# Token statistics of a conv and recurrence layer: squares summed over every eighth token, 1/rms stored without a turn by TensorE

## Chip, core and metric

The kernel runs on one core of one Trainium2 chip. The metric is device time in microseconds (us) of one execution. Before the change the median of 3 runs is 727.97 us (727.86 to 728.05). Engines are named as in the profile: PE is TensorE's matmul, PEld its weight load, DVE VectorE, ACT ScalarE, POOL GpSimd, SP SyncE, which issues most DMAs.

## What is computed

One layer over 1024 tokens of 1024 channels, batch 1. A token's 1/rms scales all channels of that token; the change lies in how this one number per token is made and spread.

```python
h = rmsnorm(x, norm_g) * (1.0 + scale) + shift      # scale, shift, gate from silu(c) @ mod_w + mod_b
u = h @ w_in                                        # five groups of 1024 columns
cv, cg, cs, lx, ls = jnp.split(u, ...)
...                                                 # gated causal conv (31 taps), layernorm, projection
...                                                 # causal conv (4 taps), gates, linear recurrence
y = jnp.concatenate([y_conv, y_lru], axis=-1) @ w_out
x = x + (1.0 + gate) * y
return rmsnorm(x, final_g)
```

with `rmsnorm(x, g) = x * rsqrt(mean(x * x, axis=-1) + EPS) * g`.

## The kernel before

Channels stand on the 128 partitions and tokens along the free dimension. x arrives as eight tiles of 128 channels x 1024 tokens (`xt[k]`). Each f32 product is made of three matmuls: both operands are split into a high part (`whi`, `uh`) and a rest (`wlo`, `ul`), and hi x hi, hi x rest and rest x hi are summed in one PSUM bank of 512 columns. Weights come by DMA (`raw`), ScalarE casts the high part (`whi`), VectorE or GpSimd subtracts for the rest (`wlo`).

The first column tiles of u don't wait for the norm. `uh`, `ul` (line 875) are x times the channel's gain alone, and the products of `first` (line 790, seven banks over four column tiles, and `late` for the eighth) and of the three tiles in `NEXT` (line 505, `ps`) are multiplied by 1/rms of the token afterwards, on VectorE, by the row `rbc` that holds the 1024 values on every partition. Those results are `first_u` (lines 1310 and 1318) and `next` (line 1359). Then VectorE scales x itself by `gs` and `rbc` (line 997), ScalarE and VectorE make the full h from it in two parts (again `uh`, `ul`, lines 1006 and 1008), and all later tiles of u read these. `fsum` (line 970) and `psbias` (line 985) make the part of u that comes from shift.

The statistics (lines 918 to 951): ScalarE squares the eight tiles of x, VectorE adds them into one tile `sq` of 128 partitions x 1024 tokens. `stats` (line 932) then sums over partitions: eight f32 matmuls, in each of which 128 token columns of `sq` are the stationary operand and a column of ones moves, so that the sums of block b stand in column b of `psb` (named token_stats), token p of the block on partition p. ScalarE takes the root (line 940, `st`, 128x8), VectorE the reciprocal (line 942). `turn` (line 944) is a matmul with `st` as stationary operand against the identity matrix: it puts block b on partition b, 8x128, in the same bank. ScalarE copies this to SBUF (line 948) and issues the DMA that stores it in DRAM as a row of 1024 in token order (line 949); SyncE issues the DMA that reads that row onto all 128 partitions, `rbc` (line 950).

The order of work isn't the program's order. `S.op` collects operations with their engine, a cost, a priority, and what they read and write; `Plan.order` (line 174) plays a list schedule over all of them with those costs and sets the order of the whole program on each engine. An operation that goes, or gets another cost or predecessor, therefore can move others anywhere behind it. On the chip only semaphores for real dependences hold; `after=` and priorities act on the order alone.

Of the kernel before, what the change touches and what calls it, by code (L numbers as in the profile page):

```python
# [9 lines left out]
F32 = mybir.dt.float32  # L10
# [4 lines left out]
P = 128  # L15
D = 1024
T = 1024
KT = D // P
# [72 lines left out]
SQP, RSP, BIP, HHP, HCH, EVP = -84, -110, -50, -56, 0.1, -80  # L91
# [25 lines left out]
class Plan:  # L117
# [14 lines left out]
    @staticmethod  # L132
    def keys(items):
        for it in items:
            if isinstance(it, tuple):
                yield it
            else:
                for i in range(it.parts):
                    yield (it, i)
# [162 lines left out]
def hymba_layer(ctx: ExitStack, tc: tile.TileContext, xT, xa, vecs, mod_w, w_first, w_pairs, w_in,  # L302
# [3 lines left out]
    act, dve, pool, pe, sp = nc.scalar, nc.vector, nc.gpsimd, nc.tensor, nc.sync  # L306
# [7 lines left out]
    dram = ctx.enter_context(tc.tile_pool(name="dram", bufs=1, space=bass.MemoryType.DRAM))  # L314
# [11 lines left out]
    S = Plan(pools)  # L326


    def a_cost(n, ptr=0):
        return 0.1 + 0.00083 * n + 0.09 * ptr  # L330
# [7 lines left out]
    def ACT(prio, out, in_, func, n=T, bias=None, scale=None, accum=None, r=(), w=(),  # L338
            reserve=0, after=()):
        kw = {}  # L340

        def emit():
            if func == "copy":
                act.copy(out(), in_())  # L344
                return
            if bias is not None:
                kw["bias"] = bias
            if scale is not None:
                kw["scale"] = scale
            if accum is not None:  # L350
                kw["accum_out"] = accum
            act.activation(out=out(), in_=in_(), func=func, **kw)  # L352
        ptr = sum(x is not None and not isinstance(x, float) for x in (bias, scale))
        return S.op("ACT", a_cost(n, ptr) + (0.1 if accum is not None else 0), emit, prio, r, w,
                    table=SETS.get(func), reserve=reserve, after=after)
# [33 lines left out]
    def DMA(prio, out, in_, nbytes, r=(), w=(), after=(), reserve=0):  # L389
        cost = max(0.1, nbytes / (EARLYRATE if prio < -94.5 + KT * 3.3 else 360e3))  # L390
        cost = FIRSTCOST.get(round(prio), cost) if prio < -96 else cost
        return S.op("SP", cost, lambda: sp.dma_start(out(), in_()), prio, r, w, after=after,
                    reserve=reserve)
# [7 lines left out]
    def big_buf(name, dt=F32, parts=1):  # L401
        return S.buf("big", name, dt, parts)

    def bank(name):
        return S.buf("bank", name)
# [5 lines left out]
    def part(b, a, e):  # L411
        if isinstance(b, Two):
            z = a // H
            return part(b.b[z], a - z * H, e - z * H)
        return lambda: b()[:, a:e]

    def halves(b, a, e):
        if isinstance(b, Two):
            return [(b.b[z], 0) for z in (0, 1) if z * H < e and a < z * H + H]
        return [(b, i) for i in range(b.parts) if i * (T // b.parts) < e  # L420
                and a < (i + 1) * (T // b.parts)]

    FULL_BYTES = P * T * 4
# [9 lines left out]
    ident = const.tile([P, P], F32, tag="ident", name="ident")  # L433
    make_identity(nc, ident)
    ones = const.tile([P, P], F32, tag="ones", name="ones")
# [6 lines left out]
    def ctile(name, n):  # L442
        return const.tile([P, n], F32, tag=name, name=name)
# [296 lines left out]
    psb = bank("token_stats")  # L740
# [16 lines left out]
    for i in range(IDLE):  # L757
        if i == IDLE0:
            for z, (a, e) in enumerate(CPARTS):
# [3 lines left out]
             after=[spread_op] if i >= IDLE0 else [])  # L763
# [9 lines left out]
    def fw_keys(b, k, a=0, e=FW):  # L773
        o, n = (k % 2) * FW, T // b.parts
        return [(b, j) for j in range((o + a) // n, (o + e - 1) // n + 1)]
# [27 lines left out]
    for i, ld in enumerate(LOADS):  # L803
        p = due[ld] = i - 100.0
# [5 lines left out]
        elif ld[0] in "wW":  # L810
# [6 lines left out]
                w=keys(rw))  # L817
            for j in range(k, k + nk):
# [3 lines left out]
                for a, e in ((0, FW // 2), (FW // 2, FW)) if j == 0 else ((0, FW),):  # L822
                    ACT(p, fw_part(hi, j, a, e), fw_part(rw, j, a, e), "copy", e - a, r=[(rw, jj)],
                        w=fw_keys(hi, j, a, e))
                if j:
                    SUB(p, "DVE", fw_part(lo, j), fw_part(rw, j), fw_part(hi, j), FW,
                        r=[(rw, jj), *fw_keys(hi, j)], w=fw_keys(lo, j))
# [31 lines left out]
    for k in range(KT):  # L859
        p = due[f"s{k}"]  # L860
# [13 lines left out]
        p = max(p, due[f"x{k}"] if k else p, due[f"w{k}"])  # L874
# [4 lines left out]
        for a, e in START if k < UK else ((0, T),):  # L879
            n = e - a  # L880
            hk = halves(x_, a, e)
            if k == 0 == a:
                o = TS(p, part(uh, a, e), part(x_, a, e), g, None, ALU.mult, n=n,
                       r=hk + [("gs", k)], w=halves(uh, a, e))
            else:
                o = ACT(p, part(uh, a, e), part(x_, a, e), AF.Copy, n, scale=g,
                        r=hk + [("gs", k)], w=halves(uh, a, e))
            if k == 0 == a:
                rw, hi, lo = fw[0]
                for b in (0, FW // 2):  # L890
                    z = b + FW // 2
                    SUB(p, "DVE", fw_part(lo, 0, b, z), fw_part(rw, 0, b, z), fw_part(hi, 0, b, z), z - b,
                        r=[(rw, 0), *fw_keys(hi, 0, b, z), *halves(uh, a, e)], w=fw_keys(lo, 0, b, z))
# [3 lines left out]
                r=hk + halves(uh, a, e) + [("gs", k)], w=halves(ul, a, e)))  # L897
# [10 lines left out]
        for ch, (a, e) in enumerate(START):  # L908
            for i, ps in enumerate(psf):
                if (a, e) not in cuts[i] or k == 0 == a:  # L910
                    continue
                q = p + 0.1 * ch if k < LASTK else due[f"w{KT - 1}"] + 0.01 * ((i + 1) % 4) + 0.001 * ch
                for z in range(3) if k < ZK else (None,):
                    o = fw_mm(q + 0.003 * (z or 0), ps, i, uh, ul, k, ((a, e),),
                              after=[begun[i, a // H]] if k == 0 and a % H else [], z=z)
# [3 lines left out]
    for k in range(KT):  # L919
        p = SQP + k  # L920
        sq = big_buf(f"sq{k}")
        ACT(p, sq, xt[k], AF.Square, r=[xt[k]], w=[sq], after=[scaled[k]])
        if k:
            to = sqs[0]
            TT(p, SUM[k], to, to, sq, ALU.add, r=[to, sq], w=[to],
               after=[last_split[k + SQD]] if k <= SQK else [])
        else:
            sqs.append(sq)
    rbc = big_buf("rbc", parts=4)
    st, wk = ctile("st", KT), [psb]  # L930

    def stats(sq, k):
        for b in range(KT):
            pe.matmul(psb()[:, b:b + 1], sq()[:, b * P:b * P + P], ones[:, 0:1],
                      start=k == 0 and b == 0, stop=k == len(sqs) - 1, skip_group_check=True)

    for k, sq in enumerate(sqs):
        S.op("PE", 0.23 * KT, lambda sq=sq, k=k: stats(sq, k), RSP, [sq], wk, columns=4 * P * KT,
             after=[last_u[LASTK - 1, 3, 0]] if k else [])
# [1 line left out]
               scale=1.0 / D, r=wk, w=[("st", 0)])  # L941
    S.op("DVE", 0.2, lambda: dve.reciprocal(st, st), RSP, [("st", 0)], [("st", 0)])

    def turn():
        pe.matmul(psb()[:KT, P:2 * P], st, ident, start=True, stop=True)
    spread = S.op("PE", 0.2, turn, RSP, [("st", 0)], wk, columns=4 * P)
    row, flat = lambda: rbc()[:KT, :P], dram.tile([KT, P], F32, tag="rrow", name="rrowd")
    spread_out = ACT(RSP, row, lambda: psb()[:KT, P:2 * P], "copy", P, r=wk, w=[(rbc, 0)])
    S.op("ACT", 0.3, lambda: act.dma_start(flat, row()), RSP, [(rbc, 0)], [("rrowd", 0)], lag=0.1)
    DMA(RSP, rbc, lambda: flat.rearrange("b p -> (b p)").partition_broadcast(P), FULL_BYTES,  # L950
        r=[("rrowd", 0)], w=[rbc])


# [4 lines left out]
    for k in range(KT):  # L958
        p = due[f"h{k}"]
# [6 lines left out]
        if k == 0:  # L966
            ACT(p, facc, fw_part(rw, k), AF.Copy, FW, scale=shift[:, k:k + 1],
                r=[(rw, 0), ("shift", k)], w=[(fsum, 0)])
# [3 lines left out]
        for i, s in enumerate(NEXT):  # L972
            to, rw = part(fsum, FW + i * P, FW + i * P + P), raw[s]
            src = lambda rw=rw, k=k: k3(rw)()[:, k, :]
            if k == 0:
                ACT(p + 5, to, src, AF.Copy, P, scale=shift[:, k:k + 1],
                    r=[(rw, k), ("shift", k)], w=[(fsum, 1)])
            else:
                STT(p + 5, to, src, shift[:, k:k + 1], to, ALU.mult, ALU.add, P,
                    r=[(rw, k), ("shift", k), (fsum, 1)], w=[(fsum, 1)])  # L980
    psx = bank("psbias")

    def shift_mm():
# [5 lines left out]
        w=[("bias", 0)])  # L989
# [3 lines left out]
    for ch, (a, e) in enumerate(START):  # L993
        for k in range(KT):
            p, n = TP + k + HCH * ch, e - a
# [38 lines left out]
    def by_two(b, a, e):  # L1034
        return lambda: part(b, a, e)().rearrange("p (m q) -> p q m", q=2)

    def apart(b, a, e):
        return lambda: b().rearrange("p (q m) -> p q m", q=2)[:, :, a // 2:e // 2]
# [262 lines left out]
    for i, (s, ps) in enumerate(zip(FIRST, psf)):  # L1301
        j, p, bi = s[1] % KT, EVP + i, bias[:, i:i + 1]
        t = big_buf(f"first_u{i}", parts=4)
        for a, e in START:
            tk, pk, n = halves(t, a, e), halves(ps, a, e), e - a
            if (a, e) in cuts[i]:
                alone = len(cuts[i]) == 1
                if alone:
                    ACT(RSP, part(t, a, e), part(ps, a, e), "copy", n, r=pk, w=tk)
                TT(p - 4 * alone, "DVE", part(t, a, e), part(t if alone else ps, a, e),  # L1310
                   part(rbc, a, e), ALU.mult, n, r=(tk if alone else pk) + halves(rbc, a, e),
                   w=tk).slack = RBC_LAG
            else:
                late = bank("late")
                for k in range(KT):
                    fw_mm(RSP + 60 + 0.1 * k, late, i, uhs[k], uls[k], k, ((a, e),),
                          after=[spread], off=a)
                TT(p, "DVE", part(t, a, e), part(late, 0, n), part(rbc, a, e), ALU.mult, n,
                   r=[late] + halves(rbc, a, e), w=tk)
            if s[1] < CG:  # L1320
                if a == 0:
                    v[j] = big_buf(f"v{j}")
                STT(p + 3, apart(v[j], a, e), by_two(t, a, e), bi, by_two(sig[j], a, e), ALU.add,
                    ALU.mult, n, r=tk + halves(sig[j], a, e) + [("bias", 0)], w=[v[j]])
        if s[1] >= CG:
            ACT(p + 3, t, t, AF.Sigmoid, bias=bi, r=[t, ("bias", 0)], w=[t])
            sig[j] = t
# [6 lines left out]
    for s in slots[4:]:  # L1334
# [31 lines left out]
        else:  # L1366
            t = big_buf(f"acc{m}", parts=2)
            DMA(n - 1, t, lambda m=m: xT[m * P:(m + 1) * P, :], FULL_BYTES, w=[t],
                after=[started[n - 2]])
            for a, e in FULL:  # L1370
                STT(n + 0.5, part(t, a, e), part(ps, a, e), gate1[:, m:m + 1], part(t, a, e),
                    ALU.mult, ALU.add, H, r=halves(ps, a, e) + halves(t, a, e) + [("gate1", m)],
                    w=halves(t, a, e))
# [8 lines left out]
    for p in range(KT // 2):  # L1382
        n = C0 + 2 * p
        early, later = PWE[p] if p else (None, None)
        w = pair_weights("pw2", p, n, last[:1] if early is None else [begun_pw2[p - early[0]][early[1]]],
                         last[1:] if later is None else [begun_pw2[p - later[0]][later[1]]], WPW[p])
# [4 lines left out]
        for m in (2 * p, 2 * p + 1):  # L1391
            t, sr = big_buf(f"yc{m}", parts=2), big_buf(f"scsr{m}", parts=2)
            DMA(n - 0.5, sr, lambda m=m: scs_d[m], FULL_BYTES, r=[("scsd", m)], w=[sr],
                after=[ops[1]])
# [4 lines left out]
        for i, a, z, (src, *more) in ps:  # L1399
            t, sr, b = ts[i], ss[i], bs[i]  # L1400
            to, sg, tk, sk = part(t, a, z), part(sr, a, z), halves(t, a, z), halves(sr, a, z)
            if more:
                STT(n + 1, to, src[0], b, more[0][0], ALU.add, ALU.add, H,
                    r=src[1] + more[0][1], w=tk)
# [5 lines left out]
        after=[begun_pw2[-1][6]])  # L1410
# [107 lines left out]
    for i, p in enumerate(OUT_P):  # L1518
        end = i == len(OUT_P) - 1
        w = pair_weights("out", p, n, last[:1], last[1:], WOUT[i])  # L1520
# [108 lines left out]
```

## Time and profile before

| | |
|---|---|
| median of 3 runs | 727.97 us |
| the profiled execution's own time | 727.94 us |
| its span, first to last instruction | 725.7 us |
| granted TensorE clock over the span | 0.998 |
| PE busy | 718.5 us, 99% |
| DVE busy | 638.8 us, 88% |
| ACT busy | 463.6 us, 64% |
| POOL busy | 97.2 us, 13% |
| DMA, mean over the span | 154 GB/s |

The profile is of one execution. Its page has the busy times, the chain of work that ended last, and the costliest groups of instructions; the trace behind it gives timelines, waits and sums by stretch. Matmuls are pipelined: a matmul of 512 columns is shown with 389 ns, but the next starts earlier, so costs on PE are read from the distance between starts. A bracket at the end of a timeline row holds the idle time ahead of the instruction and what ended it.

### The profile page before, as it was taken

What the parts mean: (1) busy time and instruction counts of PE and PEld (TensorE: products, weight loads), DVE (VectorE), ACT (ScalarE), POOL (GpSimd) and SP (SyncE); (2) the same over time, 40 slices, a digit from 0 to 9 for tenths busy, and PEclk for the clock granted to TensorE, in tenths of its full rate; (3) what the DMA queues carried; (4) which work ended last, traced back from release to release, by engine and by line L of the source; (5) the groups of instructions that cost most, each with busy time, mean ns of one, the idle gap of its engine ahead of it and who ended that gap; (6) DMA issues with size and microseconds to landing.
All of it is one profiled execution on the core that took longest, in us unless ns stands there. A gap on an engine that the chain in (4) does not pass through costs nothing.

```text
span 725.7 us, 8892 instructions
## 1 busy us (share of the span) xinstructions
PE 718.5 (99%) x3256; PEld 598.3 (82%) x3256; DVE 638.8 (88%) x911; ACT 463.6 (64%) x632; POOL 97.2 (13%) x105
## 2 busy tenths in 40 slices
PE   9999999999999999999999999999999999999996
PEld 8888888888888888888888888888888888888886
DVE  7989999999999988688899995999899766997757
ACT  6660585777777977957867985835764334645433
POOL 0042012121132332233121100000000000000001
PEclk9999999999999999999999999999999999999999
DMA  9962024387599699699784537243332530433116
GB/s 337 408 241 84 1 74 115 95 205 172 133 264 252 138 217 229 139 221 209 181 179 95 100 90 198 89 174 130 131 117 81 209 96 21 158 110 140 62 54 232
DMA packets 36490, 112.10 MB, mean 154 GB/s; under 512 B 4056, under 2 KB 10976, under 8 KB 36448
## 3 DMA queue, kind: packets, MB, share of 16 engines
q1 hardware_dynamic: 23616, 76.89, 29.9%
q0 software_dynamic: 12528, 34.26, 25.9%
q8 instruction: 25, 0.41, 0.2%
q10 hardware_dynamic: 304, 0.40, 0.2%
q14 instruction: 17, 0.14, 0.1%
HBM read 64.69 MB, written 12.59 MB: 106 GB/s over the span
## 4 chain that ended last, share of the span: by engine, by line
PE 99%; DVE 0%; DVEq 0%; issue 0%
PE ps L505 66%; PE first L790 5%; PE pbpw L616 3%; PE pupw L616 3%; PE papw L616 3%; PE gate L1220 3%; PE out L686 2%; PE puout L616 2%; PE paout L616 2%; PE pcpw L616 1%; PE pb0out L616 1%; PE pcout L616 1%; PE out6b L686 1%; PE late L790 1%; PE c_row L755 0%; PE token_stats L750 0%
## 5 line engine op out<-in xcount | busy, mean ns | idle before, releaser
L505 PE MATMUL ps<-uh,whi 128*128 128x512 f32 x576 | 224.2, 389 | 0.0
L505 PE MATMUL ps<-ul,whi 128*128 128x512 f32 x576 | 224.1, 389 | 0.0
L505 PE MATMUL ps<-uh,wlo 128*128 128x512 f32 x576 | 224.1, 389 | 0.0
L505 PEld LDWEIGHTS ps<-uh,wlo 128*128 128x128 f32 x576 | 108.1, 188 | 22.6
L505 PEld LDWEIGHTS ps<-uh,whi 128*128 128x128 f32 x576 | 108.1, 188 | 22.4
L505 PEld LDWEIGHTS ps<-ul,whi 128*128 128x128 f32 x576 | 108.1, 188 | 22.3
L344 ACT CAST whi<-raw 128x1024 fp32r<-128x1024 f32 x46 | 48.0, 1047 | 39.4 <-PE ps L505 32.6
L352 ACT ACT_TABLE_LOAD x47 | 60.3, 1283 | 3.3 <-issue 1.5
L376 POOL DMA_DIRECT2D es<-cq x45 | 39.8, 897 | 167.3 <-ACT cq L352 120.4
L371 DVE TENSOR_TENSOR wlo<-raw,whi 128x1024 fp32r<-128x1024 f32 x39 | 47.6, 1221 | 16.2 <-ACT whi L344 16.0
L363 DVE SCALAR_TENSOR_TENSOR cacc<-v,V,cacc 128x511 f32<-128x511 f32 (+14 forms) x75 | 55.7, 743 | 0.5
L363 DVE SCALAR_TENSOR_TENSOR caccs<-v,V,caccs 128x511 f32<-128x511 f32 (+6 forms) x70 | 52.1, 744 | 1.1
L363 DVE SCALAR_TENSOR_TENSOR caccs<-c,wsum,caccs 128x511 f32<-128x511 f32 (+6 forms) x70 | 52.1, 744 | 0.6
L505 PE MATMUL ps<-yh,wlo 128*128 128x512 f32 x128 | 49.8, 389 | 0.0
L505 PE MATMUL ps<-yh,whi 128*128 128x512 f32 x128 | 49.8, 389 | 0.0
L505 PE MATMUL ps<-yl,whi 128*128 128x512 f32 x128 | 49.8, 389 | 0.0
L376 POOL DMA_DIRECT2D oo<-co x42 | 37.7, 897 | 80.8 <-ACT co L352 33.1
L371 POOL TENSOR_TENSOR fg<-fg,bc 128x512 f32<-128x512 f32 x2 | 2.5, 1276 | 276.8 <-ACT bc L344 276.8
L363 DVE SCALAR_TENSOR_TENSOR xs<-ps,V,xs 128x512 f32<-128x512 f32 (+3 forms) x48 | 35.8, 746 | 0.2
L352 ACT ACTIVATE cq<-v,V 128x511 f32<-128x511 f32 (+14 forms) x45 | 31.9, 708 | 0.0
L352 ACT ACTIVATE cq<-c,wsum 128x512 f32<-128x512 f32 x42 | 29.7, 715 | 0.0
L371 POOL TENSOR_TENSOR wlo<-raw,whi 128x1024 fp32r<-128x1024 f32 x7 | 18.0, 2588 | 85.5 <-ACT whi L344 85.5
(382 smaller groups left out, 1458.9 us busy)
## 6 DMA issues: line engine op xcount, KB each, us to landing
raw<-in_w_in_dram SPq DMA_DIRECT2D x36, 512.0 KB, 5.3
modw<-in_mod_w_dram SPq DMA_DIRECT2D x24, 512.0 KB, 8.3
raw<-in_w_out_dram SPq DMA_DIRECT2D x10, 512.0 KB, 3.7
scsd<-scs SPq DMA_DIRECT2D x8, 512.0 KB, 4.0
acc<-in_xT_dram SPq DMA_DIRECT2D x8, 512.0 KB, 4.4
accd<-acc SPq DMA_DIRECT2D x8, 512.0 KB, 2.7
rawpw<-in_pw_dram SPq DMA_DIRECT2D x8, 512.0 KB, 3.4
scsr<-scsd SPq DMA_DIRECT2D x8, 512.0 KB, 5.4
```

The lines of the kernel that those rows point to most:

```text
L344: act.copy(out(), in_())
L352: act.activation(out=out(), in_=in_(), func=func, **kw)
L363: dve.scalar_tensor_tensor(out=out(), in0=in0(), scalar=scalar, in1=in1(), op0=op0, op1=op1, accum_out=accum)
L371: lambda: e.tensor_tensor(out=out(), in0=a(), in1=b(), op=op), prio, r, w,
L376: return S.op("POOL", ISSUE, lambda: pool.dma_start(out(), a(), accum_op=ALU.add), prio, r, w, lag=RATE * n / T, after=after)
L505: pe.matmul(part(ps, a - off, b - off)(), k3(lhs)()[:, k, :], rhs[k]()[:, a:b], start=(k == 0 and lhs is wh and rhs is xh and (a - off) % ...
L616: pe.matmul(part(ps, 0, c1 - c0)(), half(*lhs)()[:, j * P:j * P + P], half(*rhs)()[:, c0:c1], start=start and j == 0 and z == 0, stop=j == ...
L686: pe.matmul(part(ps, a - off, e - off)(), k3(lhs)()[:, k, :], rhs()[:, i * H + a % H:i * H + a % H + e - a], start=k == KORD[0] and lhs is ...
L790: pe.matmul(part(ps, a - off, b - off)(), fw_part(lhs, k, i * P, i * P + P)(), rhs()[:, a:b], start=k == 0 and lhs is wh and rhs is xh, st ...
L1220: pe.matmul(ps(), lhs()[:, j, :], rhs()[:, c0:c1], start=st == 0, stop=st == 2)
```

## The change

The stationary operand of the statistics' matmul b is now every eighth token, from token b, instead of block b of 128 adjacent tokens. So the sum of token 8p + b stands in row p, column b, and `st`, read row by row, is in token order. It is stored in DRAM as it is, 128 rows of 8 values, and the broadcast reads the 1024 values as before. `turn` and the copy out of PSUM are gone; the store reads `st` directly. What named the turn as a predecessor names the store now: the matmuls of `late`, and (through `spread_out`, formerly the copy) the casts of two of the three `NEXT` weights.

```diff
     def stats(sq, k):
         for b in range(KT):
-            pe.matmul(psb()[:, b:b + 1], sq()[:, b * P:b * P + P], ones[:, 0:1],
+            pe.matmul(psb()[:, b:b + 1], sq().rearrange("p (q b) -> p b q", b=KT)[:, b], ones[:, 0:1],
                       start=k == 0 and b == 0, stop=k == len(sqs) - 1, skip_group_check=True)
...
-    def turn():
-        pe.matmul(psb()[:KT, P:2 * P], st, ident, start=True, stop=True)
-    spread = S.op("PE", 0.2, turn, RSP, [("st", 0)], wk, columns=4 * P)
-    row, flat = lambda: rbc()[:KT, :P], dram.tile([KT, P], F32, tag="rrow", name="rrowd")
-    spread_out = ACT(RSP, row, lambda: psb()[:KT, P:2 * P], "copy", P, r=wk, w=[(rbc, 0)])
-    S.op("ACT", 0.3, lambda: act.dma_start(flat, row()), RSP, [(rbc, 0)], [("rrowd", 0)], lag=0.1)
-    DMA(RSP, rbc, lambda: flat.rearrange("b p -> (b p)").partition_broadcast(P), FULL_BYTES,
+    flat = dram.tile([P, KT], F32, tag="rrow", name="rrowd")
+    spread_out = S.op("ACT", 0.3, lambda: act.dma_start(flat, st), RSP, [("st", 0)], [("rrowd", 0)],
+                      lag=0.1)
+    DMA(RSP, rbc, lambda: flat.rearrange("p b -> (p b)").partition_broadcast(P), FULL_BYTES,
         r=[("rrowd", 0)], w=[rbc])
...
-                          after=[spread], off=a)
+                          after=[spread_out], off=a)
```

On TensorE, where the turn stood among the last matmuls of `first` (names are the program's, with buffer numbers; a minus marks the rows of before, a plus those of the change):

```order
 L790 MATMUL first_1_207<-uh_450,flo_367 128x512
 L790 MATMUL first_1_207<-ul_468,fhi_348 128x512
-L945 MATMUL token_stats<-ident,st 8x128
 L790 MATMUL first_0_182<-uh_450,fhi_348 128x512
 L790 MATMUL first_0_182<-uh_450,flo_367 128x512
```

Only the turn goes; the statistics' eight matmuls stay seven rows earlier, and the order is the same up to the first `ps` that reads the full h.

On ScalarE, from the root of the statistics on (`whi` are casts of weights, `rrowd` is the row in DRAM):

```order
 L344 CAST whi_521<-raw_431 128x1024
-L344 CAST whi_530<-raw_470 128x1024
-L344 COPY rbc<-token_stats 8x128
-L344 CAST whi_542<-raw_479 128x1024
-L949 DMA rrowd<-rbc 8x128
-L344 CAST whi_552<-raw_440 128x1024
-L344 CAST ghi_558<-graw_491 128x256
-L344 CAST whi_566<-raw_463 128x1024
+L945 DMA rrowd<-st 128x8
+L344 CAST whi_535<-raw_470 128x1024
+L344 CAST whi_545<-raw_440 128x1024
+L344 CAST whi_551<-raw_479 128x1024
```

The store moves ahead of two casts, the copy is gone, and the cast of `raw_440`, the second weight of `NEXT`, moves ahead of that of `raw_479`.

On VectorE, the first work that reads the broadcast row, before:

```order
L363 SCALAR_TENSOR_TENSOR fsum<-fraw_180,shift,fsum 128x512
L962 TENSOR_TENSOR shift<-macc,V 128x1
L371 TENSOR_TENSOR first_u_497<-late,rbc 128x512
L371 TENSOR_TENSOR first_u_603<-first_0_175,rbc 128x512
L371 TENSOR_TENSOR first_u_603<-first_1_204,rbc 128x512
```

and now:

```order
L363 SCALAR_TENSOR_TENSOR fsum<-fraw_180,shift,fsum 128x512
L371 TENSOR_TENSOR first_u_578<-first_0_175,rbc 128x512
L371 TENSOR_TENSOR first_u_578<-first_1_204,rbc 128x512
L371 TENSOR_TENSOR first_u_591<-first_0_177,rbc 128x512
L371 TENSOR_TENSOR first_u_591<-first_1_207,rbc 128x512
L371 TENSOR_TENSOR first_u_601<-first_0_182,rbc 128x512
L371 TENSOR_TENSOR first_u_601<-first_1_211,rbc 128x512
L371 TENSOR_TENSOR first_u_497<-late,rbc 128x512
L371 TENSOR_TENSOR first_u_497<-first_u_497,rbc 128x512
L371 TENSOR_TENSOR next_634<-ps_0_593,rbc 128x512
```

The product with `late` moves from first place behind the six products of `first`, and a small `shift` and an `fsum` move behind `next`. Behind this the orders differ by neighbours that change places: the products of x stand one earlier against `next`, the first gates on TensorE stand one group of three matmuls earlier, and SyncE's order has two swaps of weight loads. From 357 of VectorE's 886 instructions on, and from about 210 of ScalarE's 637, the order is the same as before.

## The prediction

> **What bounds the kernel now.** First the page's busy shares and its chain that ended last, then, as the third line, TensorE's waits.
>
> ```profile
> PE 718.5 (99%) x3256; PEld 598.3 (82%) x3256; DVE 638.8 (88%) x911; ACT 463.6 (64%) x632; POOL 97.2 (13%) x105
> PE 99%; DVE 0%; DVEq 0%; issue 0%
> PE token_stats L750 <- DVE ones L436: 1.1, 1, 1.1
> ```
>
> The chain is TensorE for 99% of the span, and the list of TensorE's waits has one entry, at the very start. Since a busy share can hide short waits, I take the span by stages next (length; busy time and count of PE, PEld, DVE, ACT, POOL; clock; DMA share and rate).
>
> ```profile
> 8.00:86.00 78.00, 77.94 (x352) 64.34 (x352) 73.71 (x130) 37.72 (x57) 13.25 (x6) 1.00 0.58 224
> 86.00:104.00 18.00, 18.00 (x88) 15.15 (x87) 18.00 (x33) 13.67 (x20) 0.00 (x0) 1.00 0.15 60
> 104.00:470.00 366.00, 366.00 (x1616) 303.07 (x1615) 332.25 (x444) 280.87 (x372) 80.75 (x91) 1.00 0.73 165
> 470.00:705.00 235.00, 235.00 (x1048) 194.75 (x1047) 197.53 (x264) 117.06 (x152) 0.00 (x0) 1.00 0.33 115
> ```
>
> From 8 to 705 us TensorE has no gap worth naming, at full clock. So a nanosecond that its queue gains or loses near 43 us moves the end by as much, unless another engine comes late afterwards. The second row shows where that would be: between 86 and 104 us VectorE is busy for all of 18.00 us as well.
>
> **The turn that goes.** TensorE's timeline around the statistics (start, length, instruction):
>
> ```profile
> 42.93 1.84 PE L934 MATMUL token_stats<-ones,sq 128*128 128x1 f32 x16
> 44.63 0.49 PE L790 MATMUL first<-uh,fhi 128*128 128x512 f32 x1
> 44.96 0.40 PE L790 MATMUL first<-uh,flo 128*128 128x512 f32 x1
> ...
> 45.88 0.40 PE L790 MATMUL first<-ul,fhi 128*128 128x512 f32 x1
> 46.21 0.39 PE L945 MATMUL token_stats<-ident,st 128*8 128x128 f32 x2
> 46.53 0.51 PE L790 MATMUL first<-uh,fhi 128*128 128x512 f32 x1
> 46.87 0.40 PE L790 MATMUL first<-uh,flo 128*128 128x512 f32 x1
> ...
> 54.15 0.39 PE L505 MATMUL ps<-uh,whi 128*128 128x512 f32 x1
> 54.38 0.39 PE L505 MATMUL ps<-ul,whi 128*128 128x512 f32 x1
> ```
>
> The length is of one pipelined matmul (0.39 us); what it costs is the distance between starts, 0.22 to 0.23 us for 512 columns. From 45.88 to 46.87 stand two such matmuls and the turn: 0.99 - 2 x 0.227 = **0.54 us that the turn costs**, the slow starts on both sides of it included. The matmul after the statistics has a slow start of its own (44.63 to 44.96), and that stays. This term is certain: -0.54 us.
>
> **The statistics that change.** Their eight matmuls run as 16 in 44.63 - 42.93 = 1.70 us, 106 ns each, for one moving column. That is the loading of the squares as stationary operand:
>
> ```profile
> L934 PEld LDWEIGHTS token_stats<-ones,sq x16: 188/192/192, 42.7 to 44.5; 128*128 128x128 f32 x16
> ```
>
> The loads overlap (192 ns each, 106 ns apart), but nothing covers them. The changed loads fetch as many values, each 32 bytes from the last (every eighth f32), where the old ones were adjacent. No row of this trace shows TensorE with such a step, so I bound it.
>
> - Not below 106 ns: as many columns go into the array, and adjacent values are the easiest case.
> - Upper end: everything that lies between is fetched too. 128 columns then span 1,024 words, and the moving operand of the rows at 54.15 and 54.38 streams 512 words in 227 ns, so a load would take about 453 ns, 16 x (453 - 106) = +5.5 us.
>
> The only strided rows are VectorE's, a step of two words against adjacent ones, with no difference:
>
> ```profile
> L371 DVE TENSOR_TENSOR v<-ps,sig 128x512 f32<-128x512 f32 x12 | 8.2, 685 | 6.1 <-PE ps L505 6.0
> L371 DVE TENSOR_TENSOR first_u<-first,rbc 128x512 f32<-128x512 f32 x6 | 3.7, 682 | 0.0
> L371 POOL TENSOR_TENSOR wlo<-raw,whi 128x1024 fp32r<-128x1024 f32 x7 | 18.0, 2588 | 85.5 <-ACT whi L344 85.5
> ```
>
> Two words is far from eight, so these do not decide. One thing speaks for the low end: a load takes one column in 0.83 ns (106/128), the moving stream one in 0.44 ns (227/512), so by estimate the port has about a factor of two to spare. One speaks against it: that spare is shown for adjacent words alone. The ends are a factor of four apart; neither row is nearer, and I take the middle by ratios, **twice, about 213 ns a load: +1.70 us**.
>
> [...]
>
> **Sum on TensorE.** +1.70 - 0.54 = +1.16 us.
>
> **What moves beside it.** The way from the statistics to the broadcast in the timelines of the engines, with GpSimd's subtractions of the weights and, as the last line, the time to landing from the view of tile rbc:
>
> ```profile
> 44.81 0.27 ACT L352 ACTIVATE st<-token_stats,eps_t 128x8 f32<-128x8 f32 x1 [0.78 <-PE token_stats L934]
> 45.11 0.20 DVE L942 RECIPROCAL st<-st 128x8 f32<-128x8 f32 x1 [0.16 <-ACT st L352]
> 46.09 13.14 POOL L371 TENSOR_TENSOR wlo<-raw,whi 128x1024 fp32r<-128x1024 f32 x5 [44.78 <-ACT whi L344]
> 46.86 0.25 ACT L344 COPY rbc<-token_stats 8x128 f32<-8x128 f32 x1
> 47.14 0.55 ACTq L949 DMA_DIRECT2D rrowd<-rbc  x1
> 49.69 0.33 SPq L392 DMA_DIRECT2D rbc<-rrowd  x1
> DMA to landing us min/median/max: 4.1/4.1/4.1
> ```
>
> Before, the store is issued at 47.14, SyncE sends the broadcast 2.55 us later, and it lands at 49.69 + 4.1 = 53.8. Now the store can go when the reciprocal ends, 45.31, or 47.0 if the statistics take 1.70 us longer. On ScalarE's queue it is moved ahead of two weight casts, which it delays by its 0.55 us at most. GpSimd's subtractions follow those casts and end at 59.23; the weight after the first is read when the 48 matmuls of the first, from 54.15, are through, at 65.0, so that is hidden. The copy (0.25 us) goes. The store now has 128 rows of 32 bytes instead of 8 of 512. If it took the same 2.55 us, the broadcast would land at 52.0 (unslowed loads) to 53.7. Behind it on SyncE's queue stand two loads each of mod_w and w_in, which go no later than before. VectorE's order follows suit:
>
> ```profile
> 54.35 0.69 DVE L371 TENSOR_TENSOR first_u<-late,rbc 128x512 f32<-128x512 f32 x1 [2.19 <-PE late L790]
> 54.96 3.67 DVE L371 TENSOR_TENSOR first_u<-first,rbc 128x512 f32<-128x512 f32 x6
> 58.55 1.24 DVE L371 TENSOR_TENSOR first_u<-first_u,rbc 128x512 f32<-128x512 f32 x1
> ...
> 60.55 0.69 DVE L371 TENSOR_TENSOR next<-ps,rbc 128x512 f32<-128x512 f32 x1
> ...
> 65.23 0.69 DVE L371 TENSOR_TENSOR next<-ps,rbc 128x512 f32<-128x512 f32 x1 [0.85 <-PE ps L505]
> ...
> 76.11 0.69 DVE L371 TENSOR_TENSOR next<-ps,rbc 128x512 f32<-128x512 f32 x1 [0.46 <-PE ps L505]
> ```
>
> The six products of first no longer stand behind late, which ended VectorE's wait of 2.19 us. VectorE gains up to that, but then waits for TensorE again at next (0.85 and 0.46 us before): until 76 us TensorE paces it. I cost all this at nothing. The cover is those waits, 1.31 us, and the earlier start; if the broadcast landed after about 55.5 us, VectorE would start the busy stretch late. There the cover is thin:
>
> ```profile
> 96.79 6.05 DVE L363 SCALAR_TENSOR_TENSOR ul<-x,shift,uh 128x512 fp32r<-128x512 f32 x9
> 102.88 0.39 PE L505 MATMUL ps<-ul,whi 128*128 128x512 f32 x1
> ```
>
> The last ul is written at 102.84 and read at 102.88: 0.04 us to spare. A TensorE that comes 1.16 us later gains slack; one that comes 0.54 us earlier needs VectorE to be earlier too, which the one more product that now stands ahead of a next allows. From 104 us on the two orders differ by swaps of neighbours, and meet again before half of the span; VectorE has 33.75 us idle in 104 to 470, so I add nothing.
>
> The profiled execution took 727.94 us (span 725.7 and 2.2 around it), the median is 727.97. Forecast: 727.94 + 1.16 = **729.1 us**, its own range 728.3 to 729.6 (loads of 165 to 245 ns).
>
> **Rivals.**
>
> - *The step costs nothing*, since the port's spare factor of two covers it: -0.54, 727.4. For it speaks 0.83 against 0.44 ns a column; against it, that no strided load stands in the trace. It needs VectorE to keep up between 86 and 104; if it doesn't, up to 0.54 comes back and the time is 727.9.
> - *Slower: each column of the strided load is a separate slow fetch*, at the slowest rate per value that the trace has on an engine, GpSimd's 2588/1024 = 2.53 ns: 324 ns a load, +3.5 - 0.54 = +2.9, 730.9. Place: the 16 loads at 43 us; it decides from (1.46 + 0.54 + 1.70)/16 = 231 ns a load, at which the time is 0.2% up. The full span at 453 ns gives 732.9. [...]
> - *The store of 32-byte rows lands late*: SyncE's broadcast is held, VectorE enters the 86 to 104 stretch late, and TensorE waits there, 1 us for each us past 55.5; what it gained before is swallowed. A store of 7 us instead of 2.55 with unslowed loads: 45.4 + 7 + 4.1 = 56.5, +1.0, 728.9.
> - *The new order leaves TensorE waiting* somewhere after 104 us for a weight, a gate or a bank: 1 to 2 us on top, 730 to 731. Against it: TensorE had no wait at all in 600 us.
>
> **How the numbers follow.** Forecast 0.38; no cost 0.34; slow fetch 0.17; late store 0.04; new wait 0.07. The range takes in the first three with a margin below for VectorE's luck: 727.0 to 731.4; outside lie the full-span fetch and a large new wait. 0.2% is 1.46 us, about what a measurement of this kernel can tell from no change. Faster by that would need more than the turn is worth: 0.04. Slower: the slow fetch, a part of the forecast's upper range, the new wait: 0.37. Same: 0.59.
>
> **What would show it.** The rows of line 934: distance between the 16 starts 106, 213 or over 230 ns. TensorE's start of the first ps matmul: 54.15 + 1.16 by the forecast, 53.6 if the step is free. The store's issue within 0.1 us of the reciprocal's end and the broadcast's some 2.5 us later. VectorE's first product before late. TensorE's waits: still the one at the start. A wait of TensorE for ul near 100 us, or a distance of loads outside 165 to 245 ns, would make the forecast wrong.

## The result and the profile after

The change takes 730.32 us (median of 6 runs, 730.23 to 732.39), the kernel before 727.85 us in runs on the same chip (6 runs, 727.32 to 728.05). The ratio is 1.0039, interval 1.0026 to 1.0052: 2.5 us slower. The profiled execution took 730.37 us (span 728.3), 2.43 us more than that of before.

First the busy times, TensorE's line of the waits, and the shares of the chain that ended last, of the changed kernel:

```profile
PE 721.5 (99%) x3254; PEld 601.7 (83%) x3254; DVE 636.9 (87%) x911; ACT 463.9 (64%) x631; POOL 97.4 (13%) x105
...
PE 99%; DVE 0%; DVEq 0%; issue 0%
```

```profile
PE token_stats L750 <- DVE ones L436: 1.1, 1, 1.1
```

TensorE still sets the end, and still its only wait is the one at the start. So the time came in as longer work on TensorE, not as a new wait. A table of stretches says where. After the stretch and its length stand the busy times of PE, PEld, DVE, ACT and POOL with their instructions, then the granted clock, the DMA share and GB/s. The change:

```profile
42.00:56.00 14.00, 14.00 (x56) 12.07 (x55) 8.88 (x15) 8.66 (x15) 5.89 (x3) 0.88 0.40 126
56.00:107.00 51.00, 51.00 (x234) 42.50 (x233) 48.44 (x96) 20.60 (x29) 7.42 (x4) 1.00 0.18 63
107.00:700.00 593.00, 593.00 (x2617) 490.98 (x2616) 524.95 (x698) 395.97 (x518) 80.82 (x91) 1.00 0.58 147
```

And before:

```profile
42.00:56.00 14.00, 14.00 (x71) 11.41 (x70) 11.65 (x16) 9.03 (x17) 9.91 (x4) 1.00 0.58 209
56.00:107.00 51.00, 51.00 (x234) 42.48 (x233) 49.55 (x98) 23.28 (x33) 4.89 (x4) 1.00 0.12 43
107.00:700.00 593.00, 593.00 (x2617) 490.78 (x2616) 523.24 (x696) 392.76 (x514) 79.20 (x91) 1.00 0.58 147
```

From 56 to 700 us TensorE does the same number of matmuls in the same time. All of the loss lies between 42 and 56 us: 56 matmuls where 71 were (two of the 15 are the turn's), at a mean clock of 0.88 where it was 1.00. PE's busy column is 14.00 of 14.00 in both, so it can't show this; the counts and the clock do. The timeline of PE there, of the change (start, duration, engine, line, operation):

```profile
42.88 3.74 PE L934 MATMUL token_stats<-ones,sq 128*128 128x1 f32 x16
46.48 0.47 PE L790 MATMUL first<-uh,fhi 128*128 128x512 f32 x1
...
47.47 0.39 PE L790 MATMUL first<-uh,flo 128*128 128x512 f32 x1
47.70 0.51 PE L790 MATMUL first<-ul,fhi 128*128 128x512 f32 x1
48.01 0.63 PE L790 MATMUL first<-uh,fhi 128*128 128x512 f32 x1
48.44 0.63 PE L790 MATMUL first<-uh,flo 128*128 128x512 f32 x1
...
51.00 0.51 PE L790 MATMUL first<-uh,flo 128*128 128x512 f32 x1
51.34 0.40 PE L790 MATMUL first<-ul,fhi 128*128 128x512 f32 x1
51.58 0.39 PE L790 MATMUL late<-uh,fhi 128*128 128x512 f32 x1
```

Two losses stand here. The statistics take 46.48 - 42.88 = 3.60 us instead of 1.70, 225 ns a load: **+1.90 us**. And from 1.3 us behind them on, the matmuls of 512 columns start up to 0.43 us apart instead of 0.227; the nine distances take 51.34 - 47.70 = 3.64 us, where they would take 9 x 0.227 = 2.04: **+1.60 us**. The table by stretches of 3.4 us names the cause of the second one, the granted clock of 0.50:

```profile
44.40:47.80 3.40, 3.40 (x16) 3.20 (x16) 1.15 (x7) 1.14 (x3) 0.00 (x0) 1.00 0.14 20
47.80:51.20 3.40, 3.40 (x10) 2.62 (x9) 3.40 (x3) 3.25 (x5) 3.21 (x1) 0.50 0.42 145
51.20:54.60 3.40, 3.40 (x16) 2.80 (x16) 0.83 (x2) 1.72 (x4) 1.36 (x1) 1.00 0.50 154
```

With the turn gone (-0.54) the three terms are +2.96 us. On PE, from the start of the statistics to the start of the last matmul, it is 679.37 us against 676.46: +2.91. The first `ps` starts at 57.02 us instead of 54.15. After the last matmul 0.3 us less follows (6.03 us against 6.33 to the end), which leaves the span's +2.6. This holds in every trace: 6.02 to 6.04 us in the nine without the turn, 6.33 to 6.37 in the three with it. What shortens the end is not known.

### The profile page after: what moved, and what is told of

Its sections match the earlier page's. It is cut to its first block, busy times and chain, and to the rows that moved or that the text cites. A ratio compares the mean times of both kernels' runs of the same rounds, so it can differ in the third digit from the quotient of the medians.

```text
span 728.3 us, 8888 instructions
## 1 busy us (share of the span) xinstructions
PE 721.5 (99%) x3254; PEld 601.7 (83%) x3254; DVE 636.9 (87%) x911; ACT 463.9 (64%) x631; POOL 97.4 (13%) x105
## 4 chain that ended last, share of the span: by engine, by line
PE 99%; DVE 0%; DVEq 0%; issue 0%
PE ps L505 66%; PE first L790 5%; PE gate L1217 3%; PE pbpw L616 3%; PE pupw L616 3%; PE papw L616 3%; PE out L686 2%; PE puout L616 2%; PE paout L616 2%; PE pcpw L616 1%; PE pb0out L616 1%; PE pcout L616 1%; PE late L790 1%; PE out6b L686 1%; PE token_stats L934 0%; PE token_stats L750 0%
```

## The experiments

Theory: two things cost, one after the other. From some step between its values on, a stationary operand loads at half speed (225 ns a load at 32 bytes from value to value, 106 ns adjacent); and a stretch of TensorE that holds nothing but matmuls of one column, 3.60 us long in the change, makes the clock drop by half for the next 3.4 us (0.50 from 47.82 to 51.23 us). Against the first stands that any step costs (B, where an expectation uses letters), or the step in proportion (C); against the second, that something else that the change moved (the store, the order, the missing turn) makes the clock drop, or that it is slow loads as such that do. Each kernel is compared with runs of the kernel before in the same batch (medians 728.09, 727.85 and 728.01 us).

**The step alone, turn kept.** Before, with one edit (line 934); with the turn in place the tokens are scaled by each other's values:

```diff
-            pe.matmul(psb()[:, b:b + 1], sq()[:, b * P:b * P + P], ones[:, 0:1],
+            pe.matmul(psb()[:, b:b + 1], sq().rearrange("p (q b) -> p b q", b=KT)[:, b], ones[:, 0:1],
```

> The kernel before with the strided stationary operand alone; turn, copy and store stay, so 1/rms comes in another token order (token 8p+b's value stands at b*128+p) and the tokens are scaled by each other's values. Order on all engines is that of before. Theory (strided loads cost 225 instead of 106 ns each, and the 3.6 us in which TensorE does little bring a half-clock window behind them): +1.9 for the loads, +1.6 for the clock, the turn stays: 731.4 us, granted clock 0.5 for 3.4 us from about 48 us. Rival (the clock falls for the missing turn, or the new order costs time): loads +1.9 only, 729.8 us, no half clock.

Measured: 731.28 us (731.22 to 733.76, 4 runs), ratio 1.0045, interval 1.0029 to 1.0060. Its profiled execution is the one of 733.76 us, in which the clock stayed at half for two such stretches, 46.03 to 52.86 us, so its trace is read for the mechanism and the median for the price. Loads of the statistics (PEld; duration min/median/max in ns, first and last start in us):

```profile
L934 PEld LDWEIGHTS token_stats<-ones,sq x16: 314/335/336, 42.9 to 46.4; 128*128 128x128 f32 x16
```

So the loads are as slow without the rest of the change, and the clock drops without it. The store, the order and the missing turn are not needed for either; the loads and one stretch at half clock would make 728.09 + 1.90 + 1.60 = 731.59, measured are 731.28.

**Adjacent columns, no turn, tokens put in order by the store.** The change, with line 934 as before, and the 4 KB stored as 1024 pieces of 4 bytes:

```diff
-    flat = dram.tile([P, KT], F32, tag="rrow", name="rrowd")
-    spread_out = S.op("ACT", 0.3, lambda: act.dma_start(flat, st), RSP, [("st", 0)], [("rrowd", 0)],
+    flat = dram.tile([KT, P], F32, tag="rrow", name="rrowd")
+    spread_out = S.op("ACT", 0.3, lambda: act.dma_start(flat.rearrange("b p -> p b"), st), RSP, [("st", 0)], [("rrowd", 0)],
```

> The changed kernel with adjacent blocks of 128 tokens as stationary operand again; the token order is made by the store, 1024 pieces of 4 bytes. Order on all engines is that of the change. Theory (all loss is the strided loads and the clock behind them): the turn's 0.54 us is gained, 727.3 us, loads 106 ns apart, no half clock at 48 us. Rival (the new order costs time): 728 us or more. If the store of 4-byte pieces takes over 6 us, VectorE starts late and TensorE waits for ul near 100 us: 728 or more as well, told apart by the broadcast's issue.

Measured: 731.87 us (731.07 to 732.08, 5 runs), ratio 1.0052 (1.0039 to 1.0064). The loads are back at 107 ns and the clock is 1.00 from 42 to 56 us, but the store takes long: from its issue to SyncE's broadcast, which waits for it, in the timelines of the two queues:

```profile
45.54 0.40 ACTq L945 DMA_DIRECT2D rrowd<-st  x1
...
56.29 0.33 SPq L392 DMA_DIRECT2D rbc<-rrowd  x1
```

10.75 us. What waits for it, in the timelines of VectorE and PE:

```profile
61.40 3.68 DVE L371 TENSOR_TENSOR first_u<-first,rbc 128x512 f32<-128x512 f32 x6 [11.33 <-DMA rbc<-rrowd]
```

```profile
59.01 0.39 PE L505 MATMUL ps<-uh,wlo 128*128 128x512 f32 x1
62.15 0.69 PE L505 MATMUL ps<-uh,whi 128*128 128x512 f32 x1 [2.75 <-DVE first_u L371]
62.63 0.63 PE L505 MATMUL ps<-ul,whi 128*128 128x512 f32 x1
```

TensorE waits 2.75 us for a bank of PSUM that `first_u` has to empty, and behind this wait the clock drops for 3.41 us too (0.63 us matmuls; mean clock 0.88 from 56 to 70 us). So a late store does cost, as the third rival of the prediction had it, but 40 us earlier than it said, through a bank and not through `ul`.

**Statistics twice, adjacent.** Before, with `for b in [*range(KT), *range(KT)]:` in `stats`: 16 more of the same short matmuls (1.7 us at their distance of 106 ns), no slow loads, no other change.

> The kernel before with the statistics' eight matmuls issued twice, adjacent loads, 32 in 3.4 us; the second pass writes the same sums again. Order of before. Theory (the half clock comes from over 3 us of single-column matmuls, whatever their operand's step): +1.7 for the second pass, +1.6 for a half-clock window: 731.1 us. Rival (the strided read itself brings the clock down): +1.7 only, 729.6 us, clock 1.0.

Measured: 731.11 us (731.06 to 732.89, 4 runs), ratio 1.0048 (1.0035 to 1.0062). Of the profiled execution (732.89 us, again the one with two stretches at half clock) the loads, then the stretches:

```profile
L934 PEld LDWEIGHTS token_stats<-ones,sq x32: 186/192/333, 42.8 to 46.7; 128*128 128x128 f32 x32
```

```profile
44.40:47.80 3.40, 3.40 (x23) 3.30 (x23) 1.26 (x6) 0.69 (x2) 0.00 (x0) 0.75 0.03 8
47.80:51.20 3.40, 3.40 (x9) 1.94 (x9) 3.40 (x4) 2.25 (x4) 2.81 (x1) 0.50 0.40 154
51.20:54.60 3.40, 3.40 (x13) 2.69 (x13) 3.20 (x2) 1.74 (x3) 3.18 (x2) 0.75 0.42 149
```

The loads are quick (192 ns, as before) and the clock drops all the same. It is the length of the stretch (3.90 us from start to start here), not the stride, that the clock answers to.

**The statistics in two halves.** The change, with `stats` issued as two operations of four blocks each, the second behind the first six matmuls of `first` that came after it:

```diff
-        S.op("PE", 0.23 * KT, lambda sq=sq, k=k: stats(sq, k), RSP, [sq], wk, columns=4 * P * KT,
-             after=[last_u[LASTK - 1, 3, 0]] if k else [])
+        S.op("PE", 0.23 * KT / 2, lambda sq=sq, k=k: stats(sq, k, range(KT // 2)), RSP, [sq], wk,
+             columns=2 * P * KT)
+        S.op("PE", 0.23 * KT / 2, lambda sq=sq, k=k: stats(sq, k, range(KT // 2, KT)), RSP, [sq], wk,
+             columns=2 * P * KT, after=[last_u[KT - 1, 1, 1]])
```

It was run in two versions: in the first, the first matmul doesn't clear the bank, so that the sums contain what stood there; the diff shows the second, which clears it.

> The changed kernel with the statistics in two halves of four matmuls and six matmuls of first between them; strided loads as in the change. Theory: loads stay 225 ns apart, but no window is idle enough, so no half clock: 730.3 - 1.6 + about 0.1 for one more switch between kinds of matmul = 728.8 us. Rival (the clock falls for the strided read or the order): half clock stays, 730.4 us.

> The statistics in two halves with six matmuls of first between, strided loads, with the bank cleared by the first matmul. Theory: as the earlier run in halves, 728.7 us, no half clock behind the statistics. Rival: half clock, 730.3 us.

Measured: 728.72 us (728.51 to 728.88, 10 runs), ratio 1.0009 (1.0000 to 1.0018), and 728.63 us (728.35 to 729.90, 10 runs), ratio 1.0011 (1.0001 to 1.0020). PE in the first:

```profile
43.00 1.83 PE L934 MATMUL token_stats<-ones,sq 128*128 128x1 f32 x8
44.70 0.47 PE L790 MATMUL first<-uh,fhi 128*128 128x512 f32 x1
...
46.17 1.83 PE L934 MATMUL token_stats<-ones,sq 128*128 128x1 f32 x8
47.87 0.47 PE L790 MATMUL first<-uh,fhi 128*128 128x512 f32 x1
```

The same 16 strided loads, 1.70 us for eight of them, with 1.47 us of other matmuls between; and the clock, from 42 to 56 us, is 1.00. In all 20 runs of the halves the mean clock was 0.997 to 0.999, as in the kernel before; in the change's six it was 0.993 to 0.996. This removes the second term alone: the halves are 0.62 and 0.63 us above their kernel before, the change 2.47, which makes 1.84 and 1.85 us, near the 1.60 read from the distances above, and the intervals of the ratios don't touch.

**Steps of two and of four tokens.** The change, with every second (fourth) token in a matmul, within four (two) groups; the store then has 512 pieces of 8 bytes (256 of 16). For two:

```diff
-            pe.matmul(psb()[:, b:b + 1], sq().rearrange("p (q b) -> p b q", b=KT)[:, b], ones[:, 0:1],
+            pe.matmul(psb()[:, b:b + 1], sq().rearrange("p (g q s) -> p g s q", g=4, s=2)[:, b // 2, b % 2], ones[:, 0:1],
...
-    flat = dram.tile([P, KT], F32, tag="rrow", name="rrowd")
+    flat = dram.tile([4, P, 2], F32, tag="rrow", name="rrowd")
```

> The changed kernel with a stationary operand of every second token (8 bytes from value to value); the store goes in 512 pieces of 8 bytes. [...] Theory B (any step costs the same): loads 225 ns apart, half clock, 730.3 us.

> The changed kernel with a stationary operand of every fourth token (16 bytes from value to value), store in 256 pieces of 16 bytes. [...] Theory C (cost grows with the span that is read): between, about 145 to 165 ns a load, 728 to 728.5 us without half clock.

Measured: two, 727.07 us (726.59 to 728.10, 10 runs), ratio 0.9993 (0.9984 to 1.0003); four, 730.41 us (729.96 to 731.06, 4 runs), ratio 1.0037 (1.0023 to 1.0051). The loads, of two:

```profile
L934 PEld LDWEIGHTS token_stats<-ones,sq x16: 193/196/197, 42.4 to 44.2; 128*128 128x128 f32 x16
```

And of four, with two rows of its table by stretches:

```profile
L934 PEld LDWEIGHTS token_stats<-ones,sq x16: 310/330/330, 42.4 to 45.9; 128*128 128x128 f32 x16
```

```profile
44.40:47.80 3.40, 3.40 (x13) 3.11 (x13) 1.59 (x7) 1.45 (x3) 0.17 (x1) 0.77 0.21 25
47.80:51.20 3.40, 3.40 (x12) 2.68 (x12) 3.40 (x3) 3.00 (x4) 3.06 (x1) 0.73 0.39 137
```

Distances of loads: adjacent 106 ns, 8 bytes apart 112, 16 bytes 223, 32 bytes 225. So the step is neither free nor priced by its width; it has an edge between 8 and 16 bytes. With it the clock's drop comes and goes: from 42 to 56 us the clock is 1.00 with steps of two, with steps of four it drops in the two rows above (0.77 and 0.73). The store of 512 pieces takes 7.05 us, and its broadcast lands at 55.94 us, about where the prediction let a late one begin to hurt; TensorE doesn't wait.

**Squares written in block order.** The change, with adjacent loads; ScalarE writes each square to the place where the token's block wants it:

```diff
-        ACT(p, sq, xt[k], AF.Square, r=[xt[k]], w=[sq], after=[scaled[k]])
+        ACT(p, lambda sq=sq: sq().rearrange("p (b q) -> p q b", b=KT),
+            lambda k=k: xt[k]().rearrange("p (q b) -> p q b", b=KT), AF.Square, r=[xt[k]], w=[sq],
+            after=[scaled[k]])
```

> The changed kernel with ScalarE writing the squares in the order of the blocks (token 8q+b at b*128+q), so that the loads are adjacent and the sums come in the change's order and store. Theory: ScalarE is 48% busy before 86 us and hides a slower strided write: turn gained, no strided load, 727.3 us. Rival (ScalarE's strided squares take over twice as long, uh comes late and TensorE waits before 43 us, or the last square holds the statistics): over 728 us, with waits of TensorE before 43 us.

Measured: 727.32 us (726.74 to 728.36, 11 runs), ratio 0.9995 (0.9986 to 1.0004). The squares, from the groups of the page:

```profile
L352 ACT ACTIVATE sq<-x 128x1024 f32<-128x1024 f32 x8 | 16.9, 2106 | 0.0
```

Twice the 1050 ns of before (the values are written 512 bytes apart), on an engine that has the time; the loads take 192 ns again, the clock stays at 1.00. The turn is gone and the store is the change's, so with quick loads neither brings a loss.

**The two best again**, with their own batch of the kernel before:

> The kernel of the step of two once more, for the interval. Theory: turn gained (-0.54), loads 112 instead of 106 ns (+0.09): 0.45 us under the kernel before. Rival (no gain, the earlier difference was chance): equal to it within 0.1 us.

> The kernel of the squares in the order of the blocks once more, for the interval. Theory: turn gained (-0.54), first load 0.1 us later: 0.43 us under the kernel before. Rival (no gain): equal to it within 0.1 us.

Measured: steps of two, 726.87 us (726.18 to 727.98, 11 runs), ratio 0.9984 (0.9975 to 0.9993); squares in block order, 727.44 us (727.02 to 727.98, 11 runs), ratio 0.9993 (0.9984 to 1.0002). The first is 1.14 us (0.16%) under the kernel before, clear of no change, but more than the 0.45 us expected, and the first batch had 0.78. The traces account for 0.77 to 0.79: from the start of the statistics PE's last matmul comes 0.48 us sooner, and the end behind it is 0.3 us shorter. The second can't be told from before by its times (0.57 us less); its traces show the same 0.77 us from the statistics on.

## Why the prediction was right and wrong

The forecast was 729.1 us with an own range of 728.3 to 729.6; 730.32 lies above that, in the whole range of 727.0 to 731.4, among the cases given as slower by over 0.2%, which had 0.37 against 0.59 for the same. The range reached so far for the sake of the slow fetch; that the time fell into it for another reason is luck. With the loads as measured and nothing else, the sum would have given 729.3 us. By its steps:

- **The bound.** TensorE without a gap, each ns on it near 43 us a ns at the end: it held. +2.91 us on PE came out as +2.6 of the span; the 0.3 us behind the last matmul had no term in the sum.
- **The turn, -0.54 us.** It held: with steps of two, where the clock stays up and the loads cost only 16 x (112 - 106) ns = 0.10 us more, PE's way from the statistics to its last matmul is 675.98 us against 676.46, 0.48 less, where 0.44 was due.
- **The load, 213 ns.** 225 ns: +1.90 us instead of +1.70, inside its band of 165 to 245. It was a middle between far ends, and that it came so near is luck: behind it stands an edge, which the steps of two and four tokens show: 106 ns adjacent, 112 ns at 8 bytes from value to value, 223 ns at 16, and no more than 225 at 32. What makes the edge is not shown.
- **"Sum on TensorE".** Here it failed. It added the new price of the loads to a kernel whose other matmuls keep their distance of 0.227 us. They didn't: 3.6 us of one-column matmuls brought 3.41 us at half clock, +1.60 us, which no step and no rival had. The doubled, quick statistics show that the length is enough, the halves that without it the drop is gone. Of the signs that the prediction named, the distance of the loads and the waits of TensorE came as forecast; the start of the first `ps`, 57.02 us instead of 55.31, showed the missing term.
- **The rival of the slow fetch**, 730.9 us, comes close in time only: it asked for loads of more than 231 ns, 324 by its price. They took 225, and the missing 1.6 us are not in the loads at all. A time that fits isn't a cause.
- **Store and broadcast.** The store went at 47.19 us, 0.03 behind the reciprocal's end, as said. It took 3.15 us to the broadcast instead of 2.55, which landed at 54.0, past the forecast's 53.7. That the smaller pieces cost these 0.6 us isn't shown: in other executions the same store took 2.05 to 4.13 us (last section). It is hidden, as costed: TensorE waits nowhere. The timelines of the queues, after:

```profile
46.96 0.20 DVE L942 RECIPROCAL st<-st 128x8 f32<-128x8 f32 x1 [2.25 <-ACT st L352]
47.19 0.34 ACTq L945 DMA_DIRECT2D rrowd<-st  x1
50.34 0.33 SPq L392 DMA_DIRECT2D rbc<-rrowd  x1
```

- **VectorE's order.** The six products of `first` run from 54.27 us, ahead of `late`, and the stretch before 107 us costs TensorE nothing, as forecast. There was no new wait.

```profile
54.27 1.29 DVE L371 TENSOR_TENSOR first_u<-first,rbc 128x512 f32<-128x512 f32 x2 [2.57 <-PE late L790]
55.86 2.48 DVE L371 TENSOR_TENSOR first_u<-first,rbc 128x512 f32<-128x512 f32 x4 [0.30 <-PE late L790]
58.26 0.68 DVE L371 TENSOR_TENSOR first_u<-late,rbc 128x512 f32<-128x512 f32 x1
```

What stays open: what exactly the clock counts (the last section narrows it down), why the end behind the last matmul is 0.3 us shorter without the turn, and one of the change's six runs (732.39 us). It lies 2 us above the others, with a mean clock of 0.993 against their 0.994 to 0.996; a second stretch at half clock would fit that, but there is no trace of this run.

## What to carry to other kernels

When a price on a saturated engine is worked out, ask also what the longer stretch does to the clock of the work behind it: here the second effect was nearly as large as the first (1.60 us against 1.90), and breaking the stretch in two took it away (clock 1.00 from 42 to 56 us). A stationary operand in f32 was read every second value at nearly no cost (112 ns a load against 106), every fourth at double the cost (223); where an order of tokens has to change, small steps, or an engine with time to spare (ScalarE's squares, 8.5 us more and nothing lost at the end), can carry it. Read counts of matmuls and the granted clock by stretch, since PE's busy time was 14.00 of 14.00 us in both kernels.

## What the runs showed of the hardware

The clock. In the clock's records of each trace the first stretch at full begins at 4.27 to 9.13 us, by execution, and every later change of the clock lies a whole number of 3.413 us behind it. In the change it is full from 6.86 us, half from 47.82 and full again from 51.23, 12 and 13 such steps later. So in these traces the clock changes only at the edges of windows of 3.413 us, and the windows lie otherwise in each execution. Two neighbouring windows of the change, and two of the second version of the halves (columns as in the tables by stretches above):

```profile
44.41:47.81 3.40, 3.40 (x16) 3.20 (x16) 1.15 (x7) 1.15 (x3) 0.00 (x0) 1.00 0.14 20
47.82:51.22 3.40, 3.40 (x10) 2.62 (x9) 3.40 (x3) 3.25 (x5) 3.21 (x1) 0.50 0.42 145
```

```profile
44.42:47.82 3.40, 3.40 (x16) 3.18 (x16) 3.40 (x6) 1.05 (x1) 2.12 (x1) 1.00 0.53 169
47.84:51.24 3.40, 3.40 (x16) 2.81 (x17) 2.27 (x5) 2.60 (x4) 0.64 (x2) 1.00 0.49 158
```

PE is shown busy for all of the first window in both. What differs on TensorE is how much of it the statistics' one-column matmuls fill, from the starts in the timelines: 2.08 us in the change, 1.94 in the halves. For all traces:

| kernel | one-column matmuls in the fullest window, us of 3.41 | clock of the next window |
|---|---|---|
| before | 1.19 | 1.00 |
| squares in block order, two traces | 0.94, 1.56 | 1.00 |
| adjacent, no turn | 1.71 | 1.00 |
| steps of two, two traces | 1.23, 1.79 | 1.00 |
| halves, two traces | 1.70, 1.94 | 1.00 |
| the change | 2.08 | 0.50 |
| the step alone | 3.01 | 0.50 |
| statistics twice | 3.04 | 0.50 |
| steps of four | 3.36 | 0.50 |

For such matmuls with strided loads the limit in these traces lies between 1.94 and 2.08 us of a window; the adjacent loads agree with it, up to 1.71 us without a drop and 3.04 with one. The half lasts one window where the statistics were over by then (the change, steps of four), and two where 0.65 or 0.87 us of them fell into it (the step alone, statistics twice). With 1.47 us of other matmuls between, the halves can't fill more than 3.41 - 1.47 = 1.94 us of any window. By estimate from this limit, a stretch of 3.60 us that a window's edge cuts in the middle, 1.80 us on each side, would bring no drop; no run here shows that. In the run with the late store, the 2.75 us in which TensorE waited fell into the window ahead of the drop.

PE's busy time doesn't show what the clock follows: in the window ahead of the drop in the change PE is shown busy for 3.40 of 3.40 us and PEld for 3.20, so "idle", as the expectation for the halves has it, is the author's word for the one-column matmuls. What the clock counts in a window is not shown.

The store. 4 KB from SBUF to DRAM, from the issue on ScalarE's queue to the broadcast that waits for it, by pieces, one time for each trace in the order of the kernels named:

| pieces | us | kernel |
|---|---|---|
| 8 of 512 bytes | 2.55; 1.28, 1.28 | before; the step alone, statistics twice |
| 128 of 32 bytes | 3.15; 2.05, 2.86; 3.97, 4.13 | the change; halves; squares in block order |
| 256 of 16 bytes | 4.24 | steps of four |
| 512 of 8 bytes | 7.05, 7.00 | steps of two |
| 1024 of 4 bytes | 10.75 | adjacent, no turn |

Up to 128 pieces the same store varies by a factor of two from execution to execution, so that no price of the pieces can be read. From 256 to 1024 it grows by about 8.5 ns a piece ((10.75 - 4.24) / 768, each from one trace).
